# Where the decay exponents of a state space block are formed: on TensorE in PSUM, or from rows spread by DMA

## The chip, the core and the metric

The kernel runs on one core of a Trainium2 chip. A core has five engines with queues of their own: PE (matrix multiplication), DVE (VectorE), ACT (ScalarE), POOL (GpSimd) and SP, which here only issues DMAs. Each engine works off its instructions strictly in the order of its queue: an instruction that waits holds up all that stand behind it. The metric is the device time of one execution in microseconds (us).

## The reference

One layer of a hybrid encoder on 256 tokens of width 1024, in float32: a feed forward half step, a mixer, and a second feed forward half step. In the mixer 16 attention heads (96 wide, with normed queries and keys) stand beside a state space part with 32 heads in 4 groups, which runs over the sequence in both directions in chunks of 128 tokens:

```
da = dt * a;  a_cs = cumsum(da)                  # log decay sums, per head
seg = a_cs[l] - a_cs[s]
decay = exp(where(l >= s, seg, -inf))            # lower triangle
cb = einsum('bclgn,bcsgn->bcgls', C, B)          # one per group
y_diag = einsum('bcgls,bcghls,bcsghp->bclghp', cb, decay, x * dt)
y = y_fwd + y_bwd + d_skip * x
y = rmsnorm_per_group(y * silu(z))
x = x + (sigmoid(gA) * (attn @ P_A) + sigmoid(gB) * (y @ P_B)) @ W_out
```

The kernel writes the scan as one product over all 256 tokens: for each head and direction a matrix exp(a_cs[l] - a_cs[s]) with a mask, times C.B, times x.dt.

## The kernel before, in words

Activations lie feature by token ([128, 256] tiles). Every large product is made exact enough by splitting: a weight piece of 128x1024 comes by DMA from SP's queue (`wload`, tile `raw`), ACT rounds it into `whi`, DVE takes the rest into `wlo`, and `mm3` issues three matmuls per 128x128 block. `raw`, `whi` and `wlo` have 4 buffers each (RAWB, WB). A feed forward block, a chunk of a group's input projection (`in_group`), of the branch projection (`branch`) or of the gates (`gates`) takes two pieces. A pair of attention heads takes one piece of 128x1088 (`proj`, 8 of them).

The mixer is written in units, sorted by the keys A0, DA, S0, DS, SF, F0, FS: 24 attention units (for every pair of heads `proj` and two times `head`), and for each of the 4 groups of state space heads `start`, four times `pair` and `finish`, beside the five chunks that project the next group. I call the work on one group a round. From the program order a scheduler makes one queue per engine, in which an instruction may move ahead of earlier ones that are not ready by the scheduler's reckoning; the splitting of weights is 50 steps ahead in priority. The queues are fixed when the kernel runs.

`head` is a chain over three engines: PE transposes q and k (`ps_qkT`), ACT copies them (`qk`), PE multiplies (`ps_sc`), DVE finds the maximum (`mx`), ACT forms two exponentials (`pr`), DVE divides, PE transposes (`ps_pT`), ACT copies (`pT`), and in each second head PE multiplies with v (`ps_o`).

`pair` in the state space part treats two heads. For three matrices (forward, backward, and the two blocks across the middle) PE first writes a mask into a PSUM bank by a product with the identity (`eye`, `msk`: 0 where a pair of tokens counts, -2**100 elsewhere, L672) and adds the row of log decay sums, spread over all partitions by a product with a column of a selection matrix (`sel1`, `sel2`, `st1`, `st2`, L673). ACT takes the exponential with the negated sums `nacs` as bias (L678, L680, L681: eight per pair). DVE multiplies by C.B (`cb`), and PE forms `ps_y`. Two of the eight PSUM banks (`ps_pl`) serve the exponents, three (`ps_g`) all small products, three (`ps_mm`) the projections. The tiles `E` have 4 buffers, shared with the squares `ysq` of `finish`.

When a group's last chunk is projected, ACT applies Silu to the five tiles `xz` of the group (L532); Silu and the exponential need different function tables, so that a table load (ACT_TABLE_LOAD) stands ahead of the one and of the other.

Of the kernel before, what the change touches and what calls it, by code (L numbers as in the profile page):

```python
# [8 lines left out]
F32 = mybir.dt.float32  # L9
# [6 lines left out]
P = 128  # L16
T = 256
# [55 lines left out]
def build(ctx, tc, A, out, dbg=None):  # L73
# [38 lines left out]
    def wload(src, sizes, pri=WPRI, pl=None):  # L112
        o = 0
        res = []
        for s in sizes:
            raw = rawp.tile([P, 1088], F32, tag="raw", name="raw")
            nc.sync.dma_start(raw[:, :s], src[:, o:o + s])
            hi = (pl or wp).tile([P, 1024 if pl else 1088], F32R, tag="whi", name="whi")
            lo = (pl or wp).tile([P, 1024 if pl else 1088], F32R, tag="wlo", name="wlo")
# [20 lines left out]
    def wstat(ps, pieces, xh, xl, k0, first, last):  # L140
        """ps[feature, token] += sum over the k tiles held in pieces"""
# [5 lines left out]
    def rsqrt(y, v, n):  # L147
        """y = v ** -0.5 on [P, n]"""
# [12 lines left out]
    vec = cp.tile([P, V_N], F32, name="vec")  # L161
    row = cp.tile([P, R_N], F32, name="row")
    cst = cp.tile([P, C_N], F32, name="cst")
# [13 lines left out]
    def token_sums(psp, sq, tag):  # L177
        """[token, 2]: the sum of sq[feature, token] over its features"""
# [5 lines left out]
    def token_rows(psp, r, tag):  # L184
        """[P, token]: r[token, 2] on every partition"""
# [19 lines left out]
    class Norm:  # L205
        """x * gain of each tile of x as it comes, and the sum of squares"""
# [76 lines left out]
    sel1 = cp.tile([P, 64], F32R, name="sel1")  # L283
    sel2 = cp.tile([P, 32], F32R, name="sel2")
    eye = cp.tile([P, P], F32R, name="eye")
    msk4 = cp.tile([P, 4, P], F32R, name="msk4")
    msk = (msk4[:, 2:4], msk4[:, 0:2], msk4[:, 1:3])
    aneg = cp.tile([P, 64], F32, name="aneg")

    def tables():  # L290
# [4 lines left out]
        V.tensor_copy(sel1, cst[:, C_S1:C_S1 + 64])  # L295
        V.tensor_copy(sel2, cst[:, C_S2:C_S2 + 32])
        V.tensor_copy(eye, ident)
        # 0 where a pair of tokens counts, -2**100 elsewhere
        ts(msk4[:, 0], ones, 1.0, 2.0 ** 100, ALU.subtract, ALU.mult)
        ts(msk4[:, 1], triB, 1.0, 2.0 ** 100, ALU.subtract, ALU.mult)  # L300
        ts(msk4[:, 2], triF, 1.0, 2.0 ** 100, ALU.subtract, ALU.mult)
        ts(msk4[:, 3], ones, 1.0, 2.0 ** 100, ALU.subtract, ALU.mult)
# [46 lines left out]
    def hook(f):  # L349
        if f == 0:  # L350
            nc.sync.dma_start(cst, A["cst"])
# [14 lines left out]
    with ExitStack() as es:  # L366
# [4 lines left out]
        ps_pl = es.enter_context(pool("ps_pl", NPL, space=PSUM, reuse_waits="tile"))  # L371
# [58 lines left out]
        # rotated shared key and its square sum  # L430
# [12 lines left out]
        # dt = softplus(raw + bias), log-decay sums  # L443
# [22 lines left out]
        # log-decay sums counted from the middle of the sequence outwards  # L466
# [10 lines left out]
        st1 = mp.tile([P, T], F32R, name="st1")  # L477
        st2 = mp.tile([P, T], F32R, name="st2")
        dup = m0.tile([P, 2, 2, P], F32, name="dup")
        for c in range(2):  # L480
            V.tensor_copy(dup[:, 0, c].rearrange("p (a b) -> p a b", a=2),
                          acs[:, c].unsqueeze(1).to_broadcast([P, 2, 64]))
            o = 32 * (1 - c)
            V.tensor_copy(dup[:, 1, c].rearrange("p (a b) -> p a b", a=4),
                          acs[:, c, o:o + 32].unsqueeze(1).to_broadcast([P, 4, 32]))
        pd = gbank("ps_dup")
        for i in range(2):
            for c in range(2):
                TE.transpose(pd[:, (2 * i + c) * P:(2 * i + c + 1) * P], dup[:, i, c], ident)
# [402 lines left out]
```

## Time and profile before

| | |
|---|---|
| three timed runs | 819.43, 820.02, 820.69 us (median 820.02) |
| span of the profiled execution | 817.6 us |
| first half step, about | 0 to 200 us |
| latent projections, decay sums, first group's projection, about | 200 to 256 us |
| rounds of the mixer and gates, about | 256 to 562 us |
| branches, output projection, second half step | 562 to 817.6 us |
| granted PE clock | 1.00 of full speed in all these stretches |

The profile gives one execution. The time of just that execution is not listed apart from the three runs; its span, from the first to the last instruction, is 2.4 us below their median. Rows of a timeline read: start, duration, engine, line, operation, tiles written <- read, count, and in brackets the idle time just before and what ended it. Rows of the groups read: busy time in all and mean ns of one instruction, then idle time before them.

### The profile page before, as it was taken

The numbers are of one execution on the slowest core, as the hardware profiler recorded it, in microseconds if no ns is written. First come the engines' busy times: TensorE is split into PE (matmuls) and PEld (weight loads), VectorE is DVE, ScalarE is ACT, GpSimd is POOL, SyncE is SP. The second block draws the span as 40 slices with busy tenths as digits, with TensorE's granted clock in tenths as the row PEclk, the third lists the DMA queues.
The fourth block names the chain that finished last, engine by engine and source line by source line (L and its number), as shares of the span: only waits on it lengthen the run. The fifth ranks groups of instructions, "written<-read, shape, count | busy, mean of one in ns | idle before, by whom it ended". The sixth has DMA issues, their size and how long they took to land.

```text
span 817.6 us, 16082 instructions
## 1 busy us (share of the span) xinstructions
PE 797.8 (98%) x6480; PEld 768.8 (94%) x6480; DVE 590.3 (72%) x1192; ACT 470.2 (58%) x810; POOL 0.2 (0%) x4
## 2 busy tenths in 40 slices
PE   6999999999998999999999999999999999999998
PEld 5999999999998998988989999999999999999998
DVE  6977776566797986897897578657787766666543
ACT  6755554455367659679676666557455544444342
POOL 0000000000000000000000000000000000000000
PEclk9999999999999999999999999999999999999999
DMA  7667774667235443322325414342665555554772
GB/s 259 214 212 224 222 229 136 184 184 215 63 92 171 131 131 104 106 79 92 103 85 168 154 52 154 112 146 68 223 184 178 175 184 182 185 184 131 197 206 75
DMA packets 39098, 126.61 MB, mean 155 GB/s; under 512 B 4464, under 2 KB 5872, under 8 KB 39024
## 3 DMA queue, kind: packets, MB, share of 16 engines
q1 hardware_dynamic: 38592, 124.69, 48.7%
q8 instruction: 51, 0.84, 0.4%
q10 hardware_dynamic: 432, 0.89, 0.3%
q14 instruction: 23, 0.19, 0.1%
HBM read 124.52 MB, written 1.05 MB: 154 GB/s over the span
## 4 chain that ended last, share of the span: by engine, by line
PE 86%; DVE 6%; ACT 5%; DMA 2%; issue 1%; ACTq 0%
PE ps_gu L137 10%; PE ps_gu L138 10%; PE ps_gu L136 10%; PE ps_d L136 5%; PE ps_d L137 5%; PE ps_d L138 5%; PE ps_in L137 4%; PE ps_in L138 4%; PE ps_in L136 4%; PE ps_y L690 3%; PE ps_sb L138 2%; PE ps_sb L137 2%; PE ps_sb L136 2%; PE ps_sc L603 2%; PE ps_gt L137 1%; PE ps_o L630 1%
## 5 line engine op out<-in xcount | busy, mean ns | idle before, releaser
L94 ACT ACTIVATE whi<-raw 128x1024 fp32r<-128x1024 f32 (+4 forms) x256 | 251.3, 986 | 209.0 <-PE ps_d L137 53.1
L97 DVE TENSOR_TENSOR wlo<-raw,whi 128x1024 fp32r<-128x1024 f32 (+4 forms) x256 | 289.8, 1134 | 112.1 <-ACT whi L94 111.2
L136 PE MATMUL ps_gu<-xh,whi 128*128 128x256 f32 x704 | 201.0, 285 | 7.9 <-ACT whi L94 7.9
L137 PE MATMUL ps_gu<-xl,whi 128*128 128x256 f32 x704 | 201.2, 286 | 0.5 <-DVE xl L100 0.4
L138 PE MATMUL ps_gu<-xh,wlo 128*128 128x256 f32 x704 | 200.8, 285 | 0.0
L136 PEld LDWEIGHTS ps_gu<-xh,whi 128*128 128x128 f32 x704 | 136.5, 194 | 8.2 <-ACT whi L94 8.2
L137 PEld LDWEIGHTS ps_gu<-xl,whi 128*128 128x128 f32 x704 | 136.5, 194 | 1.0 <-DVE xl L100 0.9
L138 PEld LDWEIGHTS ps_gu<-xh,wlo 128*128 128x128 f32 x704 | 136.4, 194 | 0.5 <-DVE wlo L97 0.5
L137 PE MATMUL ps_in<-xl,whi 128*128 128x256 f32 x368 | 105.3, 286 | 0.1
L138 PE MATMUL ps_in<-xh,wlo 128*128 128x256 f32 x368 | 105.0, 285 | 0.0
L136 PE MATMUL ps_in<-xh,whi 128*128 128x256 f32 x368 | 104.4, 284 | 0.0
L137 PE MATMUL ps_d<-hl,whi 128*128 128x256 f32 x352 | 99.1, 281 | 0.0
L136 PE MATMUL ps_d<-hh,whi 128*128 128x256 f32 x352 | 99.1, 281 | 0.0
L138 PE MATMUL ps_d<-hh,wlo 128*128 128x256 f32 x352 | 99.0, 281 | 0.0
L137 PEld LDWEIGHTS ps_in<-xl,whi 128*128 128x128 f32 x368 | 70.1, 191 | 0.6 <-DVE xl L100 0.3
L138 PEld LDWEIGHTS ps_in<-xh,wlo 128*128 128x128 f32 x368 | 70.1, 191 | 0.5 <-issue 0.3
L136 PEld LDWEIGHTS ps_in<-xh,whi 128*128 128x128 f32 x368 | 70.1, 191 | 0.1
L136 PEld LDWEIGHTS ps_d<-hh,whi 128*128 128x128 f32 x352 | 66.3, 188 | 0.0
L137 PEld LDWEIGHTS ps_d<-hl,whi 128*128 128x128 f32 x352 | 66.3, 188 | 0.0
L138 PEld LDWEIGHTS ps_d<-hh,wlo 128*128 128x128 f32 x352 | 66.3, 188 | 0.0
L100 DVE SCALAR_TENSOR_TENSOR xz<-ps_in,vec,xz 128x254 f32<-128x254 f32 (+1 forms) x96 | 44.8, 476 | 1.6 <-ACT xz L520 0.9
L94 ACT ACTIVATE hh<-sg 128x256 fp32r<-128x256 f32 x44 | 18.1, 415 | 45.9 <-DVE sg L97 45.9
(222 smaller groups left out, 1467.5 us busy)
## 6 DMA issues: line engine op xcount, KB each, us to landing
raw<-in_w_gu SPq DMA_DIRECT2D x86, 512.0 KB, 4.5
raw<-in_w_in SPq DMA_DIRECT2D x62, 512.0 KB, 4.4
raw<-in_w_d SPq DMA_DIRECT2D x32, 384.0 KB, 3.2
raw<-in_w_d SPq DMA_DIRECT2D x32, 320.0 KB, 3.4
raw<-in_w_sb SPq DMA_DIRECT2D x16, 512.0 KB, 4.4
raw<-in_w_qkv SPq DMA_DIRECT2D x8, 544.0 KB, 3.8
raw<-in_w_ab SPq DMA_DIRECT2D x8, 512.0 KB, 3.8
raw<-in_w_o SPq DMA_DIRECT2D x8, 512.0 KB, 4.2
```

Source lines behind the costliest of these rows:

```text
L94: S.activation(dst, src, AF.Copy, scale=scale)
L97: V.tensor_tensor(out=dst, in0=a, in1=b, op=op)
L100: V.scalar_tensor_tensor(out=dst, in0=a, scalar=s, in1=b, op0=op0, op1=op1)
L136: TE.matmul(ps, whi, xhi, start=first, stop=False)
L137: TE.matmul(ps, whi, xlo, start=False, stop=False)
L138: TE.matmul(ps, wlo, xhi, start=False, stop=last)
L603: TE.matmul(sc[:, t * T:(t + 1) * T], qk[:HD, t * P:(t + 1) * P], qk[:HD, T:2 * T], start=True, stop=True)
L630: TE.matmul(po[64 * j:64 * j + 64, :T], kv[:, kt, HG * NOPE + hh_ * 64:HG * NOPE + (hh_ + 1) * 64], st[hh_][:, kt], start=kt == 0, stop=kt ...
L690: TE.matmul(py[64 * j:64 * j + 64, a:b], st[c, d][:, hh_], M[i][:, j, a:b], start=n == 0, stop=n == 3)
```

## The change

1. **Decay sums spread by DMA.** `sel1`, `sel2`, `eye`, `msk4`, `st1` and `st2` go, with the seven DVE instructions in `tables` that made the first four, two of the four transposes of `ps_dup`, and both PE products of `pair`. The transposed sums are copied once (`acsT`) and written to a scratch tensor `scr` in HBM by two DMAs on ACT's queue. Each head then reads its 2 KB back, onto all 128 partitions, as a tile `rows` (3 buffers) by a DMA on SP's queue.
2. **Bias and clamp on GpSimd.** Four instructions per head add `nacs` and take the minimum with 0, over 256, 256, 128 and 128 columns, from `rows` into `E`.
3. **One exponential per head** of 128x768 on ACT, in place of eight per pair, and one product with `cb` per head on DVE.
4. **The mask inside C.B.** `cb` grows from 4 to 6 blocks of 128 columns; four small DVE products per group put triangles of ones and zeros into it.
5. **Buffers.** The two banks of `ps_pl` go to `ps_g` (5 now). `raw`, `whi`, `wlo` shrink from 1088 to 1024 columns, and `proj` takes two pieces (576 and 512 columns) in place of one.

The keys of the units and all other numbers stay. The diff, cut to its core:

```diff
-NMM, NPL, NG = 3, 2, 3
+NMM, NG = 3, 5
+RB = 3
...
-            raw = rawp.tile([P, 1088], F32, tag="raw", name="raw")
+            raw = rawp.tile([P, 1024], F32, tag="raw", name="raw")
...
+    scr = tc.dram_tile([32, 2, T], F32, name="scr")
...
-        for i in range(2):
-            for c in range(2):
-                TE.transpose(pd[:, (2 * i + c) * P:(2 * i + c + 1) * P], dup[:, i, c], ident)
-        copy(st1, pd[:, 0:T])
-        tt(st1[64:128], pd[64:128, 0:T], st1[64:128], ALU.subtract)
-        copy(st2, pd[:, T:2 * T])
-        tt(st2[32:64], pd[32:64, T:2 * T], st2[32:64], ALU.subtract)
+        for c in range(2):
+            TE.transpose(pd[:, c * P:(c + 1) * P], dup[:, c].rearrange("p a b -> p (a b)"), ident)
+        acsT = m0.tile([P, T], F32, name="acsT")
+        copy(acsT[0:64], pd[0:64, 0:T])
+        for d in range(2):
+            nc.scalar.dma_start(scr[:, d], acsT[32 * d:32 * d + 32])
...
-                (pw,) = wload(A["w_qkv"][g], [3 * HG * HD + 2 * HG * P])
-                ko = 3 * HG * HD
+                pw, pv = wload(A["w_qkv"][g], [3 * HG * HD, 2 * HG * P])
...
-                cb = ss.tile([P, 4, P], F32, tag="cb", name="cb", bufs=1)
-                copy(cb, pc.rearrange("p (a b) -> p a b", a=4))
+                cb = ss.tile([P, 6, P], F32, tag="cb", name="cb", bufs=1)
+                pc4 = pc.rearrange("p (a b) -> p a b", a=4)
+                copy(cb[:, 1:3], pc4[:, 1:3])
+                for i, j, m in ((0, 0, triF), (3, 3, triB), (4, 0, triB), (5, 3, triF)):
+                    tt(cb[:, i], pc4[:, j], m, ALU.mult)
...
-                for i in range(3):
-                    pp = ps_pl.tile([P, 2, T], F32, tag="pl", name="ps_pl")
-                    E = ss.tile([P, 2, T], F32, tag="E", name="E", bufs=EB)
-                    for j in range(2):
-                        h = 8 * g + 2 * p + j
-                        lh = sel1[:, 32 * i + h:32 * i + h + 1] if i < 2 else sel2[:, h:h + 1]
-                        TE.matmul(pp[:, j], eye, msk[i], start=True, stop=False)
-                        TE.matmul(pp[:, j], lh.to_broadcast([P, P]), st1 if i < 2 else st2, start=False, stop=True)
...
+                for j in range(2):
+                    h = 8 * g + 2 * p + j
+                    o = 32 + h
+                    rows = ss.tile([P, 2, T], F32, tag="rows", name="rows", bufs=RB)
+                    nc.sync.dma_start(rows, scr[h].unsqueeze(0).to_broadcast([P, 2, T]))
+                    E = ss.tile([P, 3 * T], F32, tag="E", name="E", bufs=EB)
+
+                    for a, b, d, t0, c, w in ((0, T, 0, 0, 0, h), (T, 2 * T, 1, 0, 1, o),
+                                              (2 * T, 2 * T + P, 1, 0, 0, o), (2 * T + P, 3 * T, 0, P, 1, h)):
+                        nc.gpsimd.tensor_scalar(out=E[:, a:b], in0=rows[:, d, t0:t0 + b - a],
+                                                scalar1=nacs[:, c, w:w + 1], scalar2=0.0,
+                                                op0=ALU.add, op1=ALU.min)
+                    ends[1] = S.activation(E, E, AF.Exp)
+                    tt(E, E, cb, ALU.mult)
```

What this does to the queues is seen in three places.

**First place, PE's queue behind the last projection chunk of a round** (a tile number such as ps_in_3877 counts allocations and differs between the two kernels). Before, after the last matmul of that chunk, come the four transposes of a head, eight mask and row products, and then 39 matmuls of the next group's first chunk (ps_in_4401), until the head's product ps_sc:

```order
L138 MATMUL ps_in_3877<-xh,wlo 128x256
L597 MATMUL ps_qkT<-cst,qs 96x128
L598 MATMUL ps_qkT<-cst,ka 96x128
L597 MATMUL ps_qkT<-cst,qs 96x128
L598 MATMUL ps_qkT<-cst,ka 96x128
L672 MATMUL ps_pl<-msk_93,eye 128x256
L673 MATMUL ps_pl<-st_2896,sel_90 128x256
```

Now the same head and the next one stand there with nothing of the projections between their steps:

```order
L139 MATMUL ps_in_3853<-xh,wlo 128x256
L577 MATMUL ps_qkT<-cst,qs 96x128
L578 MATMUL ps_qkT<-cst,ka 96x128
L577 MATMUL ps_qkT<-cst,qs 96x128
L578 MATMUL ps_qkT<-cst,ka 96x128
L583 MATMUL ps_sc<-qk 128x256 x2
L600 MATMUL ps_pT<-cst,pr 128x128 x4
L669 MATMUL ps_y<-E,xd 64x256 x4
L669 MATMUL ps_y<-E,xd 64x128 x4
L577 MATMUL ps_qkT<-cst,qs 96x128
L578 MATMUL ps_qkT<-cst,ka 96x128
```

What moved: the next group's first chunk stood inside the two heads and now stands behind them, behind the 30 ps_qkv products that follow. The same happens in the next round, and once more behind the eight pieces of the first branch projection (ps_sb), where the gates' first chunk is what moved.

**Second place, ACT's queue at the same point.** Before, the table for the exponential is loaded ahead of three exponentials of the state space part, and the head's own exponentials (pr) follow:

```order
L528 ACTIVATE xz<-ps_in_3877 128x512
L532 ACT_TABLE_LOAD
L532 ACTIVATE xz<-xz 128x512 x5
L94 ACTIVATE qk<-ps_qkT 96x512
L678 ACT_TABLE_LOAD
L678 ACTIVATE E<-ps_pl,nacs 128x256 x3
L612 ACTIVATE pr,sme<-ps_sc,mx,hr 128x256 x2
```

Now the head's exponentials carry the table load, and the state space exponentials come after both heads, ahead of the copies of the ps_qkv products and of the next weight piece:

```order
L509 ACTIVATE xz<-ps_in_3853 128x512
L513 ACT_TABLE_LOAD
L513 ACTIVATE xz<-xz 128x512 x5
L95 ACTIVATE qk<-ps_qkT 96x512
L592 ACT_TABLE_LOAD
L592 ACTIVATE pr,sme<-ps_sc,mx,hr 128x256 x2
```

```order
L680 ACTIVATE ysq<-yg 128x512
L661 ACTIVATE E<-E 128x768 x3
L95 ACTIVATE qs<-ps_qkv 128x192
L95 ACTIVATE kv<-ps_qkv,rk 128x256
L95 ACTIVATE whi<-raw 128x1024
L95 ACTIVATE qs<-ps_qkv 128x192
```

What moved: three exponentials of 768 columns, which wait for GpSimd, now stand ahead of the rounding of the first weight piece of the next group. That piece takes the buffer that the first of the two waiting ps_qkv weight pairs leaves.

**Third place, ACT's queue at the end of the first group's projection.** Before, the weight pieces, the copy of the last chunk and Silu follow one another. Now three exponentials stand ahead of them, and with them the way of the decay sums through HBM:

```order
L95 ACTIVATE acsT<-ps_dup 64x256
L474 DMA scr<-acsT 32x256 x2
L95 ACTIVATE whi<-raw 128x576
L95 ACTIVATE whi<-raw 128x512
L509 ACTIVATE xz<-ps_in_3132 128x512
L501 ACTIVATE xz<-ps_in_3060,vec 128x256
L661 ACTIVATE E<-E 128x768 x2
L95 ACTIVATE whi<-raw 128x576
L661 ACTIVATE E<-E 128x768
L95 ACTIVATE whi<-raw 128x512
L509 ACTIVATE xz<-ps_in_3195 128x512
L513 ACT_TABLE_LOAD
```

What moved: Silu of the first group, on which C.B and all of the first round hang, now waits for three heads' rows to be written, read back and clamped.

More of the change, by code (lines that the diff above doesn't have):

```diff
@@ L115, in wload @@
         for s in sizes:
-            raw = rawp.tile([P, 1088], F32, tag="raw", name="raw")
+            raw = rawp.tile([P, 1024], F32, tag="raw", name="raw")
             nc.sync.dma_start(raw[:, :s], src[:, o:o + s])
-            hi = (pl or wp).tile([P, 1024 if pl else 1088], F32R, tag="whi", name="whi")
-            lo = (pl or wp).tile([P, 1024 if pl else 1088], F32R, tag="wlo", name="wlo")
+            hi = (pl or wp).tile([P, 1024], F32R, tag="whi", name="whi")
+            lo = (pl or wp).tile([P, 1024], F32R, tag="wlo", name="wlo")
             with tc.high_priority(pri):
@@ L162, in build @@
     row = cp.tile([P, R_N], F32, name="row")
-    cst = cp.tile([P, C_N], F32, name="cst")
+    cst = cp.tile([P, C_S1], F32, name="cst")
     x = xp.tile([P, KD, T], F32, name="x")
@@ L294, in tables @@
         nc.sync.dma_start(row, A["row"])
[L295 to L302, printed above, removed]
         posf = sm.tile([P, 2], F32, tag="posf", name="posf", bufs=1)
@@ L350, in hook @@
         if f == 0:
-            nc.sync.dma_start(cst, A["cst"])
+            nc.sync.dma_start(cst, A["cst"][:, :C_S1])
             for k in range(KD):
@@ L698, in finish @@
                 y = st["y"]
-                sq = [ss.tile([P, 2, T], F32, tag="E", name="ysq", bufs=EB) for _ in range(2)]
+                sq = [ss.tile([P, 3 * T], F32, tag="E", name="ysq", bufs=EB)[:, 0:2 * T] for _ in range(2)]
                 for i in range(2):
-                    S.activation(sq[i], y[:, 2 * i:2 * i + 2], AF.Square)
+                    S.activation(sq[i], y[:, 2 * i:2 * i + 2].rearrange("p a b -> p (a b)"), AF.Square)
                 tt(sq[0], sq[0], sq[1], ALU.add)
-                tt(sq[0][:, 0], sq[0][:, 0], sq[0][:, 1], ALU.add)
-                pr = norm_rows(ps_g, sq[0][:, 0], 512.0, "g")
+                tt(sq[0][:, 0:T], sq[0][:, 0:T], sq[0][:, T:], ALU.add)
+                pr = norm_rows(ps_g, sq[0][:, 0:T], 512.0, "g")
                 for i in range(4):
```

41 lines of the change are left out of this document (9 added, 32 removed).

## The prediction

> **What bounds the kernel now.** I read the page's head first, then the busy times of the mixer's stretches, then PE's own rows. PE is busy nearly always:
>
> ```profile
> span 817.6 us, 16082 instructions
> PE 797.8 (98%) x6480; PEld 768.8 (94%) x6480; DVE 590.3 (72%) x1192; ACT 470.2 (58%) x810; POOL 0.2 (0%) x4
> ```
>
> Each row of the next view is a stretch of the mixer (from, to, length; then PE, weight loads, DVE, ACT and POOL busy; clock, DMA share, GB/s). The rounds from 307 to 437 leave PE under 2 us idle in 65, and DVE some 10:
>
> ```profile
> 307.00:372.00 65.00, 63.10 (x494) 56.74 (x493) 54.38 (x136) 48.03 (x102) 0.00 (x0) 1.00 0.31 99
> 372.00:437.00 65.00, 63.15 (x497) 56.96 (x496) 56.39 (x148) 47.94 (x102) 0.00 (x0) 1.00 0.30 98
> 437.00:562.00 125.00, 124.55 (x998) 115.50 (x997) 81.45 (x188) 84.24 (x163) 0.00 (x0) 1.00 0.37 119
> ```
>
> So a matmul fewer is worth time, but only what it occupies, and only if PE isn't left waiting. The little that PE waits for in the rounds comes mostly from the work that goes and from the softmax (total us, times, longest):
>
> ```profile
> PE ps_pl L672 <- ACT E L678: 2.2, 2, 1.1
> PE ps_pT L620 <- DVE pr L104: 1.5, 3, 0.8
> ```
>
> **What goes from PE.** The groups' busy times mislead, as matmuls overlap:
>
> ```profile
> L672 PE MATMUL ps_pl<-msk,eye 128*128 128x256 f32 x96 | 27.2, 310 | 2.2 <-ACT E L678 2.2
> L673 PE MATMUL ps_pl<-st,sel 128*128 128x256 f32 x96 | 24.6, 283 | 0.0
> ...
> 306.88 0.28 PE L672 MATMUL ps_pl<-msk,eye 128*128 128x256 f32 x1
> ...
> 307.47 0.28 PE L673 MATMUL ps_pl<-st,sel 128*128 128x256 f32 x1
> ```
>
> Their sum is 51.8 us, but from 306.88 to 307.47 five intervals pass, 0.118 us each. 192 x 0.118 = **22.7 us** go, 5.7 per round. The two transposes less are nothing beside it.
>
> **What PE then waits for.** Before, the chain of a head at the end of a round was covered. These rows show it: the last chunk's copy, table and Silu on ACT, the head's copy, its product on PE, maximum and scaling on DVE, exponentials on ACT, normalisation on DVE, transposes on PE.
>
> ```profile
> 307.30 0.58 ACT L528 ACTIVATE xz<-ps_in 128x512 f32<-128x512 f32 x1
> 307.90 1.28 ACT L532 ACT_TABLE_LOAD   x1
> 309.19 2.72 ACT L532 ACTIVATE xz<-xz 128x512 f32<-128x512 f32 x5
> 311.81 0.57 ACT L94 ACTIVATE qk<-ps_qkT 96x512 f32<-96x512 f32 x1
> ```
> ```profile
> 307.59 0.28 PE L136 MATMUL ps_in<-xh,whi 128*128 128x256 f32 x1
> ...
> 312.15 0.28 PE L138 MATMUL ps_in<-xh,wlo 128*128 128x256 f32 x1
> 312.44 1.13 PE L603 MATMUL ps_sc<-qk 96*128 96x256 f32 x4
> ...
> 316.76 0.61 PE L620 MATMUL ps_pT<-cst,pr 128*128 128x128 f32 x4
> ```
> ```profile
> 313.61 0.69 DVE L606 TENSOR_REDUCE mx<-ps_sc 128x2 f32<-128x512 f32 x1 [4.95 <-PE ps_sc L603]
> 314.33 0.16 DVE L100 SCALAR_TENSOR_TENSOR mx<-mx,hr 128x2 f32<-128x2 f32 x1
> ...
> 316.23 0.62 DVE L104 TENSOR_SCALAR pr<-pr,sme 128x256 f32<-128x256 f32 x2
> ```
>
> From ACT's copy at 307.30 to ps_sc at 312.44 it takes 5.1 us, and the 39 matmuls of the next group's chunk filled PE meanwhile (307.59 to 312.15). In the new queue they stand behind both heads, since `proj` now takes two of the four weight buffers: two waiting attention pairs fill all four, and the next chunk's weights must wait until the first pair's ps_qkv are done, which stand behind the heads. So these waits are on PE's path:
>
> - Silu ahead of the first copy: 5.1, less 0.5 for the transposes that PE still does: 4.6 us.
> - From the end of ps_sc (313.57) to ps_pT it was 3.2; without the 0.3 that ACT spent on other exponentials, 2.9. The table load, which stood ahead of `E`, now comes behind the maximum: +1.28. Together 4.2.
> - Before the second head's copy stands `ysq`, which waits for the buffer that ps_y leaves: 0.65 + 0.6, less 0.5 of transposes, 0.8.
> - The second head's softmax again: 2.9.
>
> That is 12.5 us at the end of the first and second rounds. At the third, four chunks of ps_sb stand between and hide Silu; there 0.7 (two copies of 0.6 less the transposes) takes the place of 4.6: 8.6. **Sum 33.6 us.**
>
> **GpSimd's price.** No row of before shows arithmetic on POOL. The nearest is the same operation on DVE, the farthest I find for a simple one is the reciprocal:
>
> ```profile
> L104 DVE TENSOR_SCALAR pr<-pr,sme 128x256 f32<-128x256 f32 x32 | 9.8, 348 | 0.2
> L104 DVE TENSOR_SCALAR diag<-cst,nr 128x128 f32<-128x128 f32 x14 | 3.4, 282 | 0.1
> L453 DVE RECIPROCAL dt_q<-dt_q 128x128 f32<-128x128 f32 x1 | 1.0, 955 | 0.0
> ```
>
> Two of 0.348 and two of 0.282 are 1.26 us per head, the lower end; 768 columns at 0.955/128 are 5.7, the upper. A gain is excluded, as the work is new. I take 1.9, one and a half times the row of the same operation. [...]
>
> **The exponentials behind the heads.** Four `E` buffers hold two pairs. The next pair can be clamped only when ps_y has read the last, so POOL starts when ps_y ends, and three exponentials stand ahead of ACT's copies and of the next weight piece. An exponential of 768 columns I put at 0.76 us, from these two rows:
>
> ```profile
> L678 ACT ACTIVATE E<-ps_pl,nacs 128x256 f32<-128x256 f32 x64 | 26.3, 478 | 2.8 <-PE ps_pl L673 2.7
> L532 ACT ACTIVATE xz<-xz 128x512 f32<-128x512 f32 x20 | 10.9, 618 | 0.0
> ```
>
> After ps_y: 3 x 1.9 on POOL, 0.76, then the copies qs and kv (0.6 from start to start) and the piece:
>
> ```profile
> 333.17 0.35 ACT L94 ACTIVATE qs<-ps_qkv 128x192 f32<-128x192 f32 x1
> ...
> 333.74 0.37 ACT L94 ACTIVATE qs<-ps_qkv 128x192 f32<-128x192 f32 x1
> ...
> 306.34 1.06 ACT L94 ACTIVATE whi<-raw 128x1024 fp32r<-128x1024 f32 x1 [1.87 <-PE ps_in L137]
> ...
> 307.43 1.23 DVE L97 TENSOR_TENSOR wlo<-raw,whi 128x1024 fp32r<-128x1024 f32 x1 [1.65 <-ACT whi L94]
> ```
>
> 5.7 + 0.76 + 0.6 + 1.06 = 8.1 us. PE has 30 ps_qkv and four sums, 4.0 at 0.118: it waits 4.1, and 1.0 more at the third matmul for `wlo`. **3 x 5.1 = 15.3 us** (9.4 at the lower price of POOL).
>
> **The start of the first round.** C.B waited for Silu; the transposes of the sums were long done:
>
> ```profile
> 242.06 0.49 PE L489 MATMUL ps_dup<-cst,dup 128*128 128x128 f32 x3
> ...
> 257.30 1.13 PE L646 MATMUL ps_cb<-xz 128*128 128x256 f32 x4 [0.88 <-ACT xz L532]
> ...
> out<-x SPq DMA_DIRECT2D x8, 128.0 KB, 3.3
> x<-in_xt SPq DMA_DIRECT2D x1, 256.0 KB, 4.2
> ```
>
> Now: 242.55, 0.4 for the copy, 3.3 for the write, 4.2 for the read of 256 KB (on the destination's side), 5.7 for three heads on POOL, 0.76, one piece of 512 columns (0.6), copy, table and one Silu (0.6 + 1.3 + 0.55): 260.0, so C.B is 2.7 later. An exponential and its table load also stand between the two pairs of qs and kv, 2.0 more before the first transposes of q. **4.7 us.**
>
> **What costs nothing.** ACT's exponentials shrink (24.3 us for 32 x 0.76 against 51.2 in the three groups of `E`); ACT is not the bound. DVE's products with `cb` stay near 32 us, the 16 masks add about 4.5, the eight further pieces under 1; under the longer rounds DVE's 56 us stay hidden. The seven dropped `tables` instructions ran beside PE in the first half step. The 32 `rows` DMAs, 8.4 MB, go where DMA is a third busy; they stand ahead of weight pieces on SP, but three lie ahead of POOL and pieces four deep.
>
> **Sum.** 817.6 - 22.7 + 33.6 + 15.3 + 4.7 - 3.7 (the two waits above, which are inside the stretches that I priced anew) = 844.8. The runs' median lies 2.4 above the span: **847 us**.
>
> **Rivals.**
> *Relief wins, faster.* The softmax of the three ends alone is 2.9 + 1.3 + 0.8 + 2.9 = 7.9 each, 23.7, just what the matmuls save. If also Silu and POOL's clamp are out of the way in time, and the chain is shorter than in the rows by over 2 us at each end, it turns: 817.6 - 22.7 + 15 = 810, 812 with the rest. For it: ACT has 27 us less to do. Against it: queue order, which ACT's relief does not move. 8%; 4% more for a balance within 0.2%, which is what measurement of this kernel can tell from no change.
> *POOL is slow.* At 5.7 per head the third exponential is 11.4 later, at three ends and at the start: 4 x 11.4 = 46, 893. Against it: the work is elementwise with one input. 10%.
> *DVE and POOL hinder each other.* If each of the 128 POOL instructions holds up a DVE instruction for its 0.3 us, DVE gains 10 us per round; with 56 + 10 of then 75, in queue order, I put a third of it on the path: 3 x 4, 859. Nothing in before can show it, POOL being idle. 18%. [...]
> *The spread is slow.* If a read of one 2 KB row onto 128 partitions takes three times 4.2, the first round starts 8 later and three buffers no longer cover a pair: about 860. 5%.
>
> **Chances.** The forecast's own sum has 55%, from 836 (POOL at its lower price, the start of the first round free) to 860 (POOL at 3 us per head: 4 x 3.3 more). Slower in all 88%, same 4%, faster 8%. The range: 822 to 872, leaving out the faster cases and most of slow POOL.
>
> **What would show it.** In the changed profile, PE should wait at ps_sc for ACT's qk (4 to 5 us, twice), at ps_pT for DVE's pr (about 4 and 3 us, three times each), at ps_in or ps_gt for whi (4 us, three times), with PE at some 775 us busy. I am wrong if PE has matmuls of the next group between ps_qkT and ps_sc there, if the waits at ps_pT sum to under 15 us, or if a head costs POOL far from 1.9 us.

## The result and the profile after

| | before | after |
|---|---|---|
| median | 819.72 us (818.62 to 820.69, 4 runs) | 944.01 us (942.15 to 947.59, 4 runs) |
| ratio to before, 95% interval | | 1.1524 (1.1502 to 1.1545) |
| span of the profiled execution | 817.6 us | 940.3 us |

The changed kernel is 124 us slower. The forecast was 847, the range up to 872. The direction and the waits that were named came as forecast; the size did not.

The head of the page of after, with the slices of POOL and of the granted PE clock (40 slices of 23.5 us):

```profile
span 940.3 us, 15865 instructions
...
PE 814.2 (87%) x6286; PEld 771.3 (82%) x6286; DVE 587.9 (63%) x1188; ACT 453.9 (48%) x721; POOL 126.2 (13%) x132
...
POOL 0000000000323306060606006070000000000000
PEclk9999999999969966986689886997999999999999
```

PE is idle for 940.3 - 814.2 = 126.1 us; before it was 817.6 - 797.8 = 19.8. And it is busy for 814.2 us, with 194 matmuls fewer, where the forecast had 817.6 - 22.7 - 19.8 = 775.1. So of the 122.7 us between the spans 106.3 are new idle time, and 39.1 more busy time than the matmuls should take, less the 22.7 saved. Of PE's longer work the stretches show the source: in the rounds PE ran for much of the time at half its clock (columns as in the prediction; the third number from the end is the clock):

```profile
320.00:400.00 80.00, 53.77 (x347) 45.06 (x346) 45.20 (x121) 39.06 (x68) 15.28 (x17) 0.79 0.31 93
400.00:480.00 80.00, 52.08 (x327) 43.39 (x326) 38.99 (x115) 33.60 (x59) 30.84 (x32) 0.74 0.28 86
480.00:560.00 80.00, 68.01 (x511) 62.27 (x509) 52.49 (x108) 41.64 (x68) 15.65 (x16) 0.92 0.39 127
```

Before, the clock stood at 1.00 in all stretches. What PE waits for after the change (total us, times, longest):

```profile
PE ps_pT L600 <- DVE pr L105: 23.4, 9, 4.1
PE ps_in L137 <- ACT whi L95: 22.1, 3, 9.3
PE ps_in L139 <- DVE wlo L98: 14.7, 9, 5.9
PE ps_sc L583 <- ACT qk L95: 13.1, 6, 5.8
PE ps_gt L137 <- ACT whi L95: 12.0, 3, 9.3
PE ps_cb L626 <- ACT xz L513: 8.1, 1, 8.1
...
PE ps_qkT L578 <- DVE ka L98: 7.5, 3, 5.8
```

The end of the first round on PE, from its timeline, shows the forecast waits in order: qk, pr, and then whi:

```profile
336.15 2.08 PE L583 MATMUL ps_sc<-qk 96*128 96x256 f32 x4 [5.75 <-ACT qk L95]
342.37 1.12 PE L600 MATMUL ps_pT<-cst,pr 128*128 128x128 f32 x4 [4.14 <-DVE pr L105]
...
351.35 0.69 PE L600 MATMUL ps_pT<-cst,pr 128*128 128x128 f32 x2 [2.86 <-DVE pr L105]
```
```profile
357.09 15.20 POOL L658 TENSOR_SCALAR E<-rows,nacs 128x256 f32<-128x256 f32 x16 [37.01 <-PE ps_y L669]
...
360.87 0.84 ACT L661 ACTIVATE E<-E 128x768 f32<-128x768 f32 x1 [2.03 <-PE ps_qkv L540]
364.48 0.84 ACT L661 ACTIVATE E<-E 128x768 f32<-128x768 f32 x1 [2.77 <-POOL E L658]
368.08 0.84 ACT L661 ACTIVATE E<-E 128x768 f32<-128x768 f32 x1 [2.77 <-POOL E L658]
370.51 0.58 PE L137 MATMUL ps_in<-xh,whi 128*128 128x256 f32 x1 [9.33 <-ACT whi L95]
...
375.99 0.41 PE L137 MATMUL ps_in<-xh,whi 128*128 128x256 f32 x1
376.20 0.41 PE L138 MATMUL ps_in<-xl,whi 128*128 128x256 f32 x1
...
377.07 0.28 PE L138 MATMUL ps_in<-xl,whi 128*128 128x256 f32 x1
377.19 0.28 PE L139 MATMUL ps_in<-xh,wlo 128*128 128x256 f32 x1
```

Three things are to be seen. The exponentials come 3.6 us apart, as GpSimd finishes one head after the other, and the piece that PE needs stands behind the third: PE waits 9.33 us. After that wait the matmuls start 0.21 us apart (375.99, 376.20) in place of 0.12 (377.07, 377.19). And this goes on for six microseconds of dense work, as the clock in slices of 2 us shows:

```profile
360.00:362.00 2.00, 1.17 (x11) 1.09 (x10) 0.24 (x2) 0.84 (x1) 2.00 (x4) 1.00 0.04 13
362.00:364.00 2.00, 0.00 (x0) 0.00 (x0) 0.00 (x0) 0.00 (x0) 2.00 (x3) 0.72 0.33 118
364.00:366.00 2.00, 0.00 (x0) 0.00 (x0) 0.00 (x0) 0.84 (x1) 2.00 (x3) 0.50 0.17 51
...
376.00:378.00 2.00, 2.00 (x16) 2.00 (x16) 0.26 (x1) 1.06 (x1) 0.00 (x0) 0.86 0.94 326
```

PE stops at about 361.2, the clock is halved at about 363, and full again at about 376.5: here the half came about 2 us after PE had stopped, and full speed about 6 us after it had started again at 370.5. In slices of 0.5 us the clock of after is 1.00 or 0.50 in 1849 of 1881; so a mean clock of 0.923 over the span makes, as an estimate, 2 x (1 - 0.923) x 940.3 = 145 us at 0.50. By the trace PE was busy in some 82 of them; half of that, 41 us, is an estimate of what its work lost, close to the 39.1.

GpSimd's price, by form, beside DVE's rounding of weights (1223 ns in both kernels):

```profile
L658 POOL TENSOR_SCALAR E<-rows,nacs 128x256 f32<-128x256 f32 x64 | 78.2, 1233 | 508.8 <-DVE wlo L98 248.9 <-PE ps_y L669 229.2 <-DMA raw<-in_w_in 30.8
L658 POOL TENSOR_SCALAR E<-rows,nacs 128x128 f32<-128x128 f32 x64 | 48.9, 774 | 0.0
```
```profile
L98 DVE TENSOR_TENSOR wlo<-raw,whi 128x1024 fp32r<-128x1024 f32 x180 | 219.9, 1223 | 100.0 <-ACT whi L95 98.3 <-PE ps_gu L138 0.5 <-PE ps_gu L139 0.5
```

A head costs GpSimd 2 x 1.233 + 2 x 0.774 = 4.0 us, twice the 1.9 of the forecast.

### The profile page after: what moved, and what is told of

The parts are those of the page before. It is cut to its first block, busy times and chain, and to the rows that moved or that the text cites. A ratio compares the mean times of both kernels' runs of the same rounds, so it can differ in the third digit from the quotient of the medians.

```text
span 940.3 us, 15865 instructions
## 1 busy us (share of the span) xinstructions
PE 814.2 (87%) x6286; PEld 771.3 (82%) x6286; DVE 587.9 (63%) x1188; ACT 453.9 (48%) x721; POOL 126.2 (13%) x132
## 4 chain that ended last, share of the span: by engine, by line
PE 32%; issue 22%; POOL 8%; DVE 3%; ACT 1%; POOLq 0%; ACTq 0%
POOL E L658 8%; PE ps_gu L138 4%; PE ps_gu L139 4%; PE ps_gu L137 4%; PE ps_d L138 2%; PE ps_d L137 2%; PE ps_d L139 2%; PE ps_gt L139 1%; PE ps_gt L138 1%; PE ps_gt L137 1%; PE ps_o L137 1%; PE ps_o L138 1%; PE ps_sb L139 1%; PE ps_o L139 1%; PE ps_sb L137 1%
## 5 line engine op out<-in xcount | busy, mean ns | idle before, releaser
L658 POOL TENSOR_SCALAR E<-rows,nacs 128x128 f32<-128x128 f32 (+1 forms) x128 | 126.0, 1003 | 508.8 <-DVE wlo L98 248.9
L137 PE MATMUL ps_in<-xh,whi 128*128 128x256 f32 x368 | 111.0, 302 | 27.0 <-ACT whi L95 22.1
L139 PE MATMUL ps_in<-xh,wlo 128*128 128x256 f32 x368 | 110.2, 299 | 14.7 <-DVE wlo L98 14.7
L138 PE MATMUL ps_in<-xl,whi 128*128 128x256 f32 x368 | 110.1, 299 | 0.1
L137 PEld LDWEIGHTS ps_in<-xh,whi 128*128 128x128 f32 x368 | 75.8, 206 | 28.3 <-ACT whi L95 22.5
L139 PEld LDWEIGHTS ps_in<-xh,wlo 128*128 128x128 f32 x368 | 75.6, 205 | 16.9 <-DVE wlo L98 16.8
L138 PEld LDWEIGHTS ps_in<-xl,whi 128*128 128x128 f32 x368 | 75.6, 205 | 0.7 <-DVE xl L101 0.3
L661 ACT ACTIVATE E<-E 128x768 f32<-128x768 f32 x32 | 27.0, 844 | 72.6 <-POOL E L658 66.5
```

What stands on the lines that cost most here:

```text
L137: TE.matmul(ps, whi, xhi, start=first, stop=False)
L138: TE.matmul(ps, whi, xlo, start=False, stop=False)
L139: TE.matmul(ps, wlo, xhi, start=False, stop=last)
L658: nc.gpsimd.tensor_scalar(out=E[:, a:b], in0=rows[:, d, t0:t0 + b - a], scalar1=nacs[:, c, w:w + 1], scalar2=0.0, op0=ALU.add, op1=ALU.min)
L661: ends[1] = S.activation(E, E, AF.Exp)
```

## The experiments

Eighteen kernels ran; e11, e13, e17 and e18 have four runs, the others two. "Idle" is the span of the profiled execution less PE's busy time, and the clock is its mean.

| label | kernel | median us | ratio to before (95%) | PE idle | clock |
|---|---|---|---|---|---|
| e1 | before, two attention pieces | 860.2 | 1.0497 (1.0467 to 1.0528) | 40.6 | 0.978 |
| e2 | after, one attention piece | 900.8 | 1.0993 (1.0912 to 1.1074) | 94.9 | 0.949 |
| e3 | after, clamp on DVE | 878.9 | 1.0726 (1.0695 to 1.0757) | 73.9 | 0.951 |
| e4 | after, waits filled | 949.2 | 1.1584 (1.1503 to 1.1664) | 97.1 | 0.950 |
| e5 | e2 and e3 together | 839.5 | 1.024 (1.021 to 1.027) | 48.7 | 0.982 |
| e6 | after, clamp half on GpSimd, half on DVE | 888.7 | 1.0841 (1.0809 to 1.0872) | 82.5 | 0.948 |
| e7 | after, clamp a pair earlier | 947.0 | 1.1551 (1.1518 to 1.1585) | 126.8 | 0.918 |
| e8 | e7 with one piece | 898.8 | 1.0963 (1.0931 to 1.0995) | 95.5 | 0.949 |
| e9 | e7, exponentials held back | 904.6 | 1.1031 (1.1009 to 1.1054) | 95.0 | 0.948 |
| e10 | e9 with one piece | 862.6 | 1.0519 (1.0464 to 1.0574) | 60.8 | 0.970 |
| e11 | before, mask in C.B, clamp on DVE | 845.5 | 1.0304 (1.0285 to 1.0323) | 43.5 | 0.982 |
| e12 | e10 with the clamp on DVE | 829.3 | 1.0113 (1.0093 to 1.0134) | 38.6 | 0.988 |
| e13 | e1, waits filled | 854.5 | 1.0428 (1.0411 to 1.0446) | 28.2 | 0.994 |
| e14 | e12, clamp half on GpSimd | 837.8 | 1.0226 (1.0204 to 1.0248) | 45.0 | 0.981 |
| e15 | e12, clamp on ACT | 826.6 | 1.0089 (1.0067 to 1.0111) | 36.8 | 0.986 |
| e16 | e12, clamp half DVE, half ACT | 826.1 | 1.0083 (1.0063 to 1.0103) | 36.7 | 0.990 |
| e17 | e16, chunks earlier | 843.3 | 1.0302 (1.0285 to 1.032) | 47.4 | 0.978 |
| e18 | e16, chunks spread | 825.4 | 1.0076 (1.0061 to 1.0091) | 34.3 | 0.986 |

**First: buffers, GpSimd, clock (e1 to e4).** The buffers' part alone, in the kernel before:

```diff
-            raw = rawp.tile([P, 1088], F32, tag="raw", name="raw")
+            raw = rawp.tile([P, 1024], F32, tag="raw", name="raw")
...
-                (pw,) = wload(A["w_qkv"][g], [3 * HG * HD + 2 * HG * P])
+                pw, pv = wload(A["w_qkv"][g], [3 * HG * HD, 2 * HG * P])
```

> The kernel before, with one edit: the attention weights of a pair of heads come in two pieces of 576 and 512 columns and all weight buffers are 1024 wide, as after the change. Mask and row products stay on PE, GpSimd does nothing. Theory A (weight buffers): the next group's first chunk again falls behind the two heads at the end of a round, only the mask and row products of the state space part stand between their steps. PE then waits at ps_sc and ps_pT at three places, together 15 to 30 us, and at some of them the granted clock falls below 1.00; time 835 to 870 us. Rival B (all of the loss is GpSimd's work and the wait for it): within 1% of before, 812 to 828 us.

860.2, in the first range. Nothing but the cut of one weight piece into two makes the old kernel some 40 us slower, without GpSimd and without rows by DMA. Its PE waits at the two places that the forecast named:

```profile
PE ps_sc L602 <- ACT qk L94: 8.4, 3, 4.3
PE ps_pT L619 <- DVE pr L104: 8.4, 7, 2.7
```

The reverse, in the changed kernel; to make room in SBUF, `rows` has two buffers and the diagonal tile of the norms shares one with the squares:

```diff
-RB = 3
+RB = 2
...
-                pw, pv = wload(A["w_qkv"][g], [3 * HG * HD, 2 * HG * P])
+                (pw,) = wload(A["w_qkv"][g], [3 * HG * HD + 2 * HG * P])
```

> The kernel after, with the attention weights in one piece of 1088 columns again (to make room, the rows have 2 buffers instead of 3, and the diagonal tile of the norms shares a buffer with their squares). Theory A: the 39 or so matmuls of the next group stand inside the heads again; the 23 us of waits at ps_pT and most of the 13 us at ps_sc go, and with shorter waits most of the slow clock (39 us of PE time); the waits for GpSimd's three heads (cb 8 us, whi 34 us) stay in part: 840 to 880 us. Rival B: the loss stays with GpSimd, 910 to 945 us.

900.8, between the two ranges: 43.2 us come back, about what e1 cost, and the larger part stays. The two edits that make room are in e5, e8, e10, e12 and e14 to e18 too, and were never run by themselves.

```diff
-                        nc.gpsimd.tensor_scalar(out=E[:, a:b], in0=rows[:, d, t0:t0 + b - a],
+                        V.tensor_scalar(out=E[:, a:b], in0=rows[:, d, t0:t0 + b - a],
```

> The kernel after, with bias and clamp on DVE instead of GpSimd (the same four instructions per head), nothing else. By DVE's rows of the same operation a head costs 1.0 to 1.3 us there instead of the 4.0 measured on GpSimd. Theory A+B (both causes add): the waits at ps_in, ps_gt and ps_cb for ACT's whi and Silu, 42 us, fall to under 20, the softmax waits at ps_pT (23 us) stay; DVE has 32 to 40 us more; 890 to 925 us. If GpSimd were the only cause: 830 or less. If the weight buffers alone: 935 or more.

878.9, below the range of two causes: the clamp's engine alone is worth 65.1 us, more than the range allowed.

For the clock, unread matmuls in the waits of after (10 of 192 columns behind the transposes, 5 behind the scores, 16 ahead of the next chunk), with one of `ps_g`'s banks for their output:

```diff
+                if g in (1, 3, 5) and NF[h]:
+                    warmup(ka[:, 0, h], qs[:, 0], NF[h])
...
+                if g in (1, 3, 5):
+                    warmup(qk[:HD, 0:P], qk[:HD, T:2 * T], NS)
...
+                if g < 3:
+                    warmup(ones, y[:, 3], NY)
```

> The kernel after, with matmuls that nobody reads put into three of the waits of PE at each of the three ends of rounds: 10 behind the first head's transposes, 5 behind each ps_sc, 16 behind ps_sum (some 20 us of PE per end at full clock); they write a PSUM bank taken from ps_g (4 instead of 5). Theory C (a PE that waits a few us is granted half the clock, and runs its next 20 to 30 matmuls at 0.21 instead of 0.12 us): mean clock over the rounds rises from about 0.83 to over 0.95, and the time falls by 15 to 40 us although PE has 60 us more to do: 905 to 930 us. Rival D (the low clock has another cause, or costs nothing because the others are waited for anyway): 940 or more.

949.2, in the range of the rival. The clock rose from 0.923 to 0.950, the time did not fall. Three groups of rows give the filling 21.5 + 16.1 + 10.2 = 47.8 us of PE; PE's other work took 853.0 - 47.8 = 805.2 in place of 814.2, idle time fell by 29. So the filling was longer than the waits it filled, and the bank is another change. PE's other work became 9 us shorter, but what the half clock costs in time can't be read from this run; e13 asks again.

**Do the causes add up (e5), and what is it about GpSimd (e6 to e8)?** e5 has both edits above.

> The change with one attention piece of 1088 columns and with the clamp on VectorE, both at once. If the two causes found so far (weight buffers, worth 43.2 us alone; clamp on GpSimd, worth 65.1 us alone) act apart and add up: 944.0 - 43.2 - 65.1 = 836 us, 825 to 850. If they are two names for the same stretches (what one gives back the other gives back too): near the better of the two, 865 to 880. If these two are all that costs and the dropped matmuls (22.7 us) come through beyond them: 797 to 815.

839.5 against a sum of 836: the two causes act apart, within a few us.

```diff
-                        nc.gpsimd.tensor_scalar(out=E[:, a:b], in0=rows[:, d, t0:t0 + b - a],
+                        (nc.gpsimd if j else V).tensor_scalar(out=E[:, a:b], in0=rows[:, d, t0:t0 + b - a],
```

> The change with the clamp of the first head of each pair on VectorE and that of the second on GpSimd, so that the two run side by side. If the cost goes with the time that GpSimd takes: half of the 65.1 us comes back, 911 us (900 to 922). If it is the queue of two heads on GpSimd ahead of the second exponential that costs (8 us per pair, now 4 beside VectorE's work): nearly all comes back, 878 to 895. If any use of GpSimd beside VectorE costs (the two hindering each other): hardly anything, 930 to 945.

888.7, in the second range: with half of GpSimd's work 55 of the 65 us are back. So the cost goes neither with GpSimd's time in all nor with any use of it beside DVE. That fits one head queued behind the other; the run doesn't separate what stands behind the exponentials from what stands behind the `rows` DMAs (e10).

e7 takes the lines of `rows` and of the clamp out of `pair` into a function that is called a pair earlier:

```diff
+            def ahead(p):
...
                 BT, CT = xz[0][:, 0], xz[0][:, 1]
+                ahead(0)
...
+                if p < 3:
+                    ahead(p + 1)
```

> The change with the rows and the clamp of a pair issued one pair earlier (of the first pair at the start of the group), the exponentials where they were; GpSimd does the same 126 us of work. If the cost is that exponentials wait in ScalarE's queue for GpSimd and hold up the copies behind them: most of the 65.1 us comes back, 870 to 895 us. If the cost is GpSimd's own work (its time, or what it takes from VectorE): no change, 935 to 950.

> One attention piece and the clamp issued one pair ahead, on GpSimd. If the wait of the exponentials is GpSimd's whole cost and adds to that of the buffers: 825 to 850 us, as with the clamp on VectorE, perhaps less, since VectorE is spared 24 us. If GpSimd's own work is what costs: 895 to 905, as with one piece alone.

947.0 and 898.8, in the ranges for GpSimd's own work. But the edit did not do what it was meant to: the scheduler moved the exponentials up with the clamp, and they waited for GpSimd as before. ACT's waits in after and in e7:

```profile
ACT E L661 <- POOL E L658: 66.5, 23, 4.8
```
```profile
ACT E L667 <- POOL E L657: 70.4, 25, 4.7
```

So these two runs decide nothing; the exponentials must be held.

**The exponentials held back (e9, e10).**

```diff
-                    ends[1] = S.activation(E, E, AF.Exp)
+                    with tc.issue_after(ends[0].ins):
+                        ends[1] = S.activation(E, E, AF.Exp)
```

> As the run with the clamp one pair ahead, and the exponentials queued on ScalarE behind the softmax exponentials of the attention head that is written before the pair (in the run before they stood again right behind the clamp and waited 70.4 us for GpSimd, as in the change itself, 66.5 us). GpSimd's work is the same 126 us. If exponentials that wait in ScalarE's queue for GpSimd are the cost: their waits fall below 25 us and the time to 880-905 us. If GpSimd's own work or VectorE beside it is the cost: 935 to 950 although the waits are gone.

904.6: 42 us less than e7 with the same work on every engine, and in ACT's group of exponentials no idle time is left ahead of them (last number):

```profile
L668 ACT ACTIVATE E<-E 128x768 f32<-128x768 f32 x32 | 25.1, 836 | 0.0
```

> The same on top of one attention piece (900.8 us). If the queue on ScalarE is GpSimd's cost: 840 to 865 us, as with the clamp on VectorE (839.5). If GpSimd's own work is: 890 to 905.

862.6 (858.9 and 866.2), 36 less than e8: about the same again without the buffers' waits. It doesn't reach the 839.5 of DVE. The views of the waits of SP's queue and of ACT in e10 say what is late now:

```profile
SPq L653 <- POOL E L658: 142.1, 30, 9.8
```
```profile
ACT whi L95 <- DMA raw<-in_w_in: 31.7, 14, 5.3
ACT whi L95 <- DMA raw<-in_w_qkv: 16.2, 2, 11.0
```

A `rows` DMA stands in SP's queue and waits until GpSimd has read the buffer; the weight transfers stand behind it. The timeline of e10 between the first round and the second group's C.B:

```profile
358.12 0.32 SPq L653 DMA_DIRECT2D rows<-scr  x1
358.53 0.38 SPq L118 DMA_DIRECT2D raw<-in_w_qkv  x1
359.01 7.88 SPq L118 DMA_DIRECT2D raw<-in_w_in  x4
364.10 1.11 ACT L95 ACTIVATE whi<-raw 128x1088 fp32r<-128x1088 f32 x1 [10.96 <-DMA raw<-in_w_qkv]
...
366.50 0.58 PE L137 MATMUL ps_in<-xh,whi 128*128 128x256 f32 x1 [9.58 <-ACT whi L95]
```

The weights are issued 0.4 us after the last `rows`, and PE waits 9.58 us for them. The same view has 6.8 us in all for `in_w_in` before and 3.3 after. That the rest of GpSimd's price comes through SP's queue is read from these rows, not shown: a run with `rows` on another queue wasn't made.

**The same with DVE, and one part alone (e12, e11).** e12 has e10's edits with the clamp on DVE.

> One attention piece, the clamp on VectorE, and the exponentials queued behind the softmax exponentials. The run without the last was 839.5 us. If the exponentials' place in ScalarE's queue costs there too: 815 to 830 us. If the waits left are of attention alone: 834 to 845.

829.3: the place of the exponentials costs 10 us there too. So not all of the 42 and 36 us is GpSimd's. With one piece GpSimd cost 900.8 - 839.5 = 61 us against DVE while the exponentials stood where they were, and 862.6 - 829.3 = 33 us once they were held: holding them takes away somewhat less than half of GpSimd's price. e12 is still above before. e11 puts only the mask into C.B of the kernel before; the row products stay, the clamp reads them from PSUM:

```diff
-                        TE.matmul(pp[:, j], eye, msk[i], start=True, stop=False)
-                        TE.matmul(pp[:, j], lh.to_broadcast([P, P]), st1 if i < 2 else st2, start=False, stop=True)
+                        TE.matmul(pp[:, j], lh.to_broadcast([P, P]), st1 if i < 2 else st2, start=True, stop=True)
...
+                            ts(E[:, j, a:b], pp[:, j, a:b], w, 0.0, ALU.add, ALU.min)
+                    ends[1] = S.activation(E, E, AF.Exp)
```

> The kernel before with one part of the change: the mask inside C.B, 96 mask matmuls dropped (96 x 0.118 = 11.3 us of TensorE), row matmuls and weight pieces as before, the clamp on VectorE out of PSUM (no GpSimd, no rows by DMA), one exponential per tile. If dropped matmuls come through where the work beside them is not lengthened on a queue that TensorE waits for: 805 to 815 us, faster than before. If the clamp between row matmul and exponential costs as much as the matmuls save: 816 to 824. If it uncovers waits as in the change: over 830.

845.5, the third range. 11.3 us of matmuls go, and the time is 26 us longer: PE idles 43.5 - 19.8 = 23.7 more, and its work takes 802.5 where 797.8 - 11.3 = 786.5 were due. Without GpSimd, spread or cut weights, the mask in C.B with a clamp on DVE between product and exponential is dearer than the mask on PE.

**The clock by itself (e13).** In e1, filled with matmuls that write into the bank of the awaited product:

```diff
+                if g in (1, 3) and h == 0:
+                    for _ in range(16):
+                        TE.matmul(sc[:HD, 0:192], ka[:, 0, h], qs[:, 0], start=True, stop=True)
...
+                if g in (1, 3) and h == 1:
+                    for _ in range(8):
+                        TE.matmul(pp[:, 0:T], qk[:HD, 0:P], qk[:HD, T:2 * T], start=True, stop=True)
```

> The kernel before with two weight pieces (860.2 us), and unread matmuls in the waits at the end of the first two rounds: 16 of 192 columns behind the query and key transposes of the first head, 8 of 256 columns behind its second head's scores, written into the bank that the awaited matmuls then overwrite. They replace about 3 us of a wait of 4.25 and 2 us of one of 2.67, and leave the chain of work alone. In the run without them the granted clock stood at 0.50 from 313 to 326 us, after the first of these waits, and TensorE was busy 19.5 us longer than in the kernel before. If the half clock after a wait costs time of its own: 842 to 854 us. If it is only a companion of waits on ScalarE and VectorE: 857 to 864.

854.5, half a microsecond above the first range and below the second. The page and the filling's two groups:

```profile
PE 824.5 (97%) x6576; PEld 785.9 (92%) x6576; DVE 590.2 (69%) x1200; ACT 471.9 (55%) x818; POOL 0.2 (0%) x4
```
```profile
L603 PE MATMUL ps_sc<-qs,ka 128*96 128x192 f32 x64 | 10.7, 326 | 0.0
L622 PE MATMUL ps_pT<-qk 96*128 96x256 f32 x32 | 7.2, 379 | 0.0
```

The work itself takes 824.5 - 17.9 = 806.6 us, 10.7 less than in e1 (817.3), while the clock rose from 0.978 to 0.994. Idle fell by 12.4 for 17.9 of filling, so 5.5 of the gain were given back. The half clock has a price of its own, 6 us measured and some 11 if the filling had cost nothing, of e1's 40. Another 8.8 us of longer work (806.6 against 797.8) were not taken away; the rest of the 40 is idle time.

**Who should clamp (e14 to e16), and where the chunks stand (e17, e18).** e14 shares between DVE and GpSimd as e6 did. e15 has ACT form Relu of the negative argument and then the exponential of its negative:

```diff
+                        S.activation(E[:, a:b], rows[:, d, t0:t0 + b - a], AF.Relu, scale=-1.0, bias=acs[:, c, w:w + 1])
...
+                        ends[1] = S.activation(E, E, AF.Exp, scale=-1.0)
```

> One attention piece, exponentials held back, and the clamp shared: first head of a pair on VectorE, second on GpSimd. All on VectorE gave 829.3 us, all on GpSimd 862.6. If VectorE's load is the last limit (it is busy 65 to 68 us of 80 in the rounds, and TensorE waits 9.0 us for wlo): 816 to 827. If 4 us of GpSimd behind each other still come late: 830 to 846.

> The same with the clamp on ScalarE (Relu of minus the argument, then the exponential of minus that), none on VectorE or GpSimd: VectorE is spared 24 us, ScalarE gets 128 instructions of 0.25 to 0.45 us, 32 to 58 us. If VectorE is the last limit and ScalarE has room (it is busy 47 to 49 us of 80): 815 to 827. If ScalarE's queue is the tighter one (the copies stand in it): 835 to 860.

> The same with the first head's clamp on VectorE and the second's on ScalarE. If the load is what counts, between the two engines: 815 to 827 us. If each queue counts by itself: between the run with all on VectorE (829.3) and that with all on ScalarE.

837.8, 826.6 and 826.1. Half of the clamp on GpSimd (e14) is 8 us worse than none, which fits SP's queue. e15 and e16 lie in the ranges that were stated for load as the limit, but at their slow end, and the intervals of e12, e15 and e16 overlap: taking the clamp off DVE brings 3 us at most, within the noise of two runs. Load isn't shown to be what is left; if it is a part, it is a small one. The last two change the keys of e16:

```diff
-F0, FS = 0.3821, 0.0646
+F0, FS = 0.30, 0.0646
```

> The run with the clamp shared between VectorE and ScalarE (826.1 us), with the next group's weight chunks written earlier in each round (key 0.30 in place of 0.3821). In the program's order every attention head of the first rounds then has chunk matmuls inside it. If the waits that are left (17 us over the kernel before, and 12 us of half clock with them) come from where the chunks stand: 800 to 818 us, faster than the kernel before. If they come from the load of VectorE and ScalarE: 822 to 832.

> The same with the chunks from key 0.30 on and spread over a quarter of a round (0.25 in place of 0.0646). If the chunks' place decides: another time than the run with 0.30 alone by over 4 us. If load decides: 820 to 832 for both.

In e18 FS is 0.25 besides. 843.3 and 825.4: e17 missed both of its ranges, and the gain that was hoped for with it. e18 differs from e17 by 18 us, as expected if the chunks' place decides. So the place matters much (17 us from e16 to e17, the wrong way), and neither place beat the kernel before. No version here did; the best is 0.8% slower than before.

## Why the prediction was wrong, point by point

- **The matmuls that go, -22.7.** Right as a count: 194 fewer on the page, two of them transposes. The 22.7 us by themselves were never seen in the time: even without both causes (e12) PE's work took 788.5, not 775.1.
- **The uncovered heads, +33.6.** Right. The softmax was put at 3 x (4.2 + 2.9) = 21.3, measured 23.4; the copies at 2 x 4.6 + 3 x 0.8 + 0.7 = 12.3, measured 13.1. e1 shows the cause by itself, and e2 takes it back: 40 and 43 us in time. In e1 that is 20.8 us more idle time and 19.5 us of longer work; the second was not in the forecast.
- **GpSimd's price, 1.9 us per head.** This step failed: it is 4.0. With it the wait for whi at each of the three ends became 9.3 in place of 4.1, and the wait for C.B 8.1 in place of 0.9 + 2.7. But in the prediction's own working, three heads at four places, 2.1 us more per head are 25 us: 872, the top of the range. This term alone would not have put the time outside it; 70 of the 95.5 us that the span was off lie in the next two points.
- **Where the exponentials wait.** Only nine at the ends and the start's three were priced. This step failed too: the waits within the rounds were put at nothing. In the trace 23 of 32 wait for GpSimd, 66.5 us on ACT, and PE waits within the rounds and the gates too: for wlo 14.7 + 3.8 us where 3 were forecast, for ka 7.5, for whi some 6 beside the three ends. e9 shows that the place in the queue counts: the same work, queued so that no exponential waits, takes 42 us less, of which some 10 come with DVE as well (e5 to e12).
- **PE at full speed.** This step was missing, and it is the largest part of the sum below. The sum let PE's work take what it took in a trace with the clock at 1.00, though it put waits of over 4 us into PE's path eight times. PE's work came out 39.1 us longer, about the 41 that the time at half clock would make it. How much of it is time that would not have been waited for otherwise is open; in e13 10.7 us of the 19.5 went, and 6 us of time with them.
- The terms and the page close: idle was forecast at 844.8 - 775.1 = 69.7 and is 126.1, busy at 775.1 and is 814.2; 56.4 + 39.1 = 95.5, the whole error of the span. Of the 56.4, some 25 go with GpSimd's price as the prediction would have counted it, and some 31 are waits that it had not counted.
- **The rivals.** "POOL is slow" (893) was the nearest. The price measured lies between mine and its own, and in its own working would have given 872; it took no account of the clock either. "DVE and POOL hinder each other" is not seen in DVE's instructions, wlo taking 1223 ns as before; it is seen in GpSimd's (1.31 against 1.14 us for 128x256, last section), where it is a small part of the 4.0 us. Relief never won, nor does it in e5, e12 or e11. The spread was not slow: a read of `rows` landed 3.2 us after its issue (median), against the 4.2 of the forecast.
- **Open.** Why e12, e15, e16 and e18, without both causes, still stand 6 to 10 us above before with 22.7 us less to do. PE idles 34 to 39 us there against 19.8, in small waits, and its work takes 12 to 15 us longer than 775. Most of the second is half clock again: by the mean clock, (1 - 0.988) x 827 = 10 us in e12, and 8 to 12 in the others, an estimate. What makes the small waits isn't known: e15 and e16 leave little to engine load, and that the order was worked out for the kernel before is a guess. Nor was the part isolated that GpSimd's hold on SP's queue has in after itself, or in the 33 us between e10 and e12.

## What to carry to other kernels

Work that is moved to an idle engine costs by what waits for it in other queues, not by the idle engine's share of the span: here 13% busy cost 65 us (after against e3). When a change takes filler away from the busiest engine, price the waits, and price a lower clock after them (in after it stood at 0.50 from 363 to 376.5 us; in e12 no wait of PE in the mixer was longer than 2.7 us, and the clock from 320 to 400 us was still 0.94 on average, against 1.00 before), and put a priced range on an operation that no trace has shown. An edit made only for room (a weight piece cut in two, so that two waiting units hold all four buffers) cost 40 us by itself.

## What the runs showed of the hardware

- GpSimd needed on average 1233 ns for an add and minimum of 128x256 and 774 for 128x128. DVE's rows for the same instructions in e12 have 347 and 279:

```profile
L658 DVE TENSOR_SCALAR E<-rows,nacs 128x256 f32<-128x256 f32 x64 | 20.9, 347 | 5.6 <-DMA rows<-scr 4.4 <-PE ps_y L679 0.8
L658 DVE TENSOR_SCALAR E<-rows,nacs 128x128 f32<-128x128 f32 x64 | 16.4, 279 | 0.0
```

- Exponentials behind it, with DVE idle, came 3.6 us apart (360.87, 364.48, 368.08 in after). By the means above a head is 4.0 us.
- GpSimd's instructions took longer beside DVE's. In after its 128x256 instructions took 1.14 us on average where no TENSOR_TENSOR of DVE ran beside them and 1.31 where one did, at most 2.26 (128x128: 0.71 and 0.91). DVE's wlo of 128x1024 took 1.22 us on average both with GpSimd at work beside it (32 of 180) and without. In e9 GpSimd's averages are 1331 and 973 ns; DVE's wlo has 1225 there.
- PE's clock took its half about 2 us after PE stopped at 361 and came back 6 us after it started. Waits of 4 us were enough, as in e1 after one of 4.25 (0.50 from 314 to 326 us). In e12 the longest wait in the mixer was 2.7 us, and the clock was 0.94 on average from 320 to 400 us. In e16 PE waited 2.24 us until 347.83 and was busy for 1.76 of the five microseconds from 345, and the clock was 0.69 on average from 350 to 355 us.
